# Deferred residual tails, joined super-tile halves and early loads in a two-layer encoder kernel on eight cores

## The chip, the cores and the metric

One Trainium2 chip, all eight cores, two sequences of the batch on each. A time is the device time of the slowest core, in microseconds (us). The kernels here have a second, slower state in some of their executions: the cores of one die or of both show a lower granted clock, and the time grows by some per cent. The granted clock is what the profile gives under that name, as a share of TensorE's full clock in a stretch. It is not low wherever PE is busy: from 1010 to 1200 us, in a dense FFN stretch of a fast run of the kernel before, it was 1.00 on each of the eight cores, with 217 ns a matmul (190.00 us for 874, core 5). An interval in brackets is a 95% interval. In profiles PE is TensorE, which does the matmuls, PEld its weight loads, DVE VectorE, ACT ScalarE, POOL GpSimd and SP the engine that issues the loads and stores.

## The reference

Two layers over x of 16 x 2048 x 1024. Layer 0 mixes tokens by windowed attention with rotary positions, layer 1 by a short gated convolution. Each is followed by a gated MLP ("FFN" below) whose gate goes through a width-3 convolution over positions. Every sub-layer has an RMSNorm before it and one after it, ahead of the residual add.

```python
def _dwconv3(x, w):                       # neighbours on both sides
    xp = jnp.pad(x, ((0, 0), (1, 1), (0, 0)))
    return xp[:, :-2] * w[0] + xp[:, 1:-1] * w[1] + xp[:, 2:] * w[2]

def _short_conv_mixer(h, w_in, conv_w, w_out):
    b_gate, c_gate, xv = jnp.split(h @ w_in, 3, axis=-1)
    return (b_gate * _dwconv3(c_gate * xv, conv_w)) @ w_out

def _conv_glu_ffn(h, w_gate_up, conv_w, w_down):
    g, u = jnp.split(h @ w_gate_up, 2, axis=-1)
    return (jax.nn.silu(_dwconv3(g, conv_w)) * u) @ w_down

def reference(x, positions, ...):
    ...
    for i in range(2):
        hn = _rmsnorm(h, g_pre_mix)
        mix = attention or conv mixer of hn           # cut
        h = h + _rmsnorm(mix, g_post_mix)
        f = _conv_glu_ffn(_rmsnorm(h, g_pre_ffn), ...)
        h = h + _rmsnorm(f, g_post_ffn)
    return h
```

## The kernel before

`h` of one sequence stays on chip as 8 channel tiles of 128 x 2048, float32. Work after attention goes in two halves ("super-tiles") of 1024 positions. A small scheduler records every instruction with the buffers it reads and writes, in program order, and turns that into semaphore waits; each engine gets its own instructions in that order. In the traces it also runs them so: in the kernel before the 32 VectorE instructions of a residual tail, from 944.85 to 967.33 us, alternate multiply and add as the program does. Weights stream through a ring of six slots, loaded by POOL. PSUM, the memory that matmuls write, is used as eight banks (`banks` in the kernel): six rotate (`poolA`) for products, banks 6 and 7 (`poolB`) serve norm sums. A super-tile begins with a barrier of all engines and queues, POOL's weight loads included:

```python
def barrier():
    toks = [...]                        # last instruction of PE, ACT, DVE; every DMA
    for e_ in ENGS:                     # all five, POOL too
        e_._waits(toks)

def proj_postnorm(units_fn, nk, mov, movB, xbuf, l, gj, st):
    ...
    for m in range(NCH):                # output blocks: matmuls, squares, copies
        ...
    for sub in range(2):                # the residual tail
        ...                             # rs = exp(-0.5 ln(mean square + eps))
        for m in range(NCH):
            hv = h[:, m, s0 + sub * 512: s0 + sub * 512 + 512]
            op(DVE, f_tt(xv[m][sub], xv[m][sub], rs.ap[:, :], ALU.mult), ...)
            op(DVE, f_tt(hv, hv, xv[m][sub], ALU.add), ...)
```

The width-3 convolution needs one position beyond the half, the "halo". The first half computes it as a one-column matmul beside each pair of 512-column ones. All eight halo slots are columns of bank 6 and share one buffer, so that a write waits for the last read of any of them:

```python
halo_slots = [Item(banks[6].ap[:, i:i + 1]) for i in range(8)]
for hs in halo_slots:
    hs.buf = banks[6].buf

def proj_halo(slot, hn, hnB, hc, with_halo=True):
    b0, b1 = poolA.next(), poolA.next()
    ...
    for k in range(NCH):
        w = slot.ap[:, k * 128:(k + 1) * 128]
        op(PE, f_mm(b0.ap[:, :], w, hn[k][:, 1:513], ...), ...)
        op(PE, f_mm(b1.ap[:, :], w, hn[k][:, 513:1025], ...), ...)
        if with_halo:
            op(PE, f_mm(hi.ap, w, hn[k][:, hc:hc + 1], ...), ..., [hi.buf])
    return b0, b1, hi
```

The gated convolution and the FFN, cut to the order of their instructions:

```python
def conv_layer():
    for st in range(2):
        barrier()
        ...
        hc = norm_super(l, 0, st, hn, hnB)
        for m in range(8):
            sx, sc, sb = ring_load(...), ring_load(...), ring_load(...)
            x0, x1, xh = proj_halo(sx, hn, hnB, hc, with_halo=(st == 0))
            ...                                     # ACT copies x0, x1, xh into xs
            c0, c1, ch = proj_halo(sc, hn, hnB, hc, with_halo=(st == 0))
            cx = cx_pool.next()
            op(DVE, f_tt(cx.ap[:, 1:513], c0.ap[:, :], xs.ap[:, 1:513], ALU.mult), ...)
            op(DVE, f_tt(cx.ap[:, 513:1025], c1.ap[:, :], xs.ap[:, 513:1025], ALU.mult), ...)
            if st == 0:
                op(DVE, f_tt(cx.ap[:, hc:hc + 1], ch.ap, xs.ap[:, hc:hc + 1], ALU.mult), ...)
                ...
            y = y_pool.next()
            conv3(y.ap, cx.ap, ...)
            b0, b1, _ = proj_halo(sb, hn, hnB, hc, with_halo=False)
            op(DVE, f_tt(yb[m][:, 0:512], y.ap[:, 0:512], b0.ap[:, :], ALU.mult), ...)
            op(DVE, f_tt(yb[m][:, 512:1024], y.ap[:, 512:1024], b1.ap[:, :], ALU.mult), ...)
        proj_postnorm(..., st)

def ffn_phase(l):
    for st in range(2):
        barrier()
        ...
        hc = norm_super(l, 2, st, hn, hnB)
        for j in range(NFF):                        # 22 column blocks
            ...                                     # gate and up products, ACT copies, conv3
            op(ACT, f_act(sl.ap[:, :], gc.ap[:, :], AF.Silu), ...)
            op(DVE, f_tt(actv[j][:, 0:512], sl.ap[:, 0:512], u0.ap[:, :], ALU.mult), ...)
            op(DVE, f_tt(actv[j][:, 512:1024], sl.ap[:, 512:1024], u1.ap[:, :], ALU.mult), ...)
        proj_postnorm(units_fn, NFF, actv, actB, xbuf, l, 3, st)
```

The softmax here doesn't subtract the row's maximum and nothing guards it: scores larger than these inputs give would overflow.

Of the kernel before, what the change touches and what calls it, by code (L numbers as in the profile page):

```python
# [15 lines left out]
NCH = 8  # L16
DFF = 2816
NFF = 22
# [176 lines left out]
def build_program(n_seq=2, stop_after=None, dbg_cols=0):  # L195
# [23 lines left out]
    SCRB = 112640  # L219
    with contextlib.ExitStack() as es:  # L220
# [75 lines left out]
        def barrier():  # L296
            toks = []
            for e_ in ENGS[:3]:
                if e_.cnt > 0:
                    toks.append((e_.sem, e_.cnt))  # L300
            for d in all_dsems:
                if d.cnt > 0:
                    toks.append((d.sem, d.cnt))
            for e_ in ENGS:
                e_._waits(toks)
# [4 lines left out]
        def norm_cols(src, srcB, gl, gj, dst, dstB, n):  # L310
            ssb = poolB.next()
# [13 lines left out]
        def proj_postnorm(units_fn, nk, mov, movB, xbuf, l, gj, st):  # L325
            s0 = st * 1024
            xv = [[xbuf[:, (m * 1024 + sub * 512):(m * 1024 + sub * 512 + 512)] for sub in range(2)]
                  for m in range(NCH)]
            xB = [[Buf() for _ in range(2)] for _ in range(NCH)]
            ssb = [banks[6], banks[7]]  # L330
# [8 lines left out]
            for m in range(NCH):  # L339
                slots = units_fn(m)  # L340
# [19 lines left out]
            while pend:  # L360
                flush(pend.pop(0))
            for sub in range(2):
                rs = rs_pool.next()
                op(ACT, f_act(rs.ap[:, :], ssb[sub].ap[:, :], AF.Ln, scale=1.0 / D, bias=epst[:, 0:1]),
                   [ssb[sub].buf, constB], [rs.buf])
                op(ACT, f_act(rs.ap[:, :], rs.ap[:, :], AF.Exp, scale=-0.5), [rs.buf], [rs.buf])
                tt = 2 * st + sub
                for m in range(NCH):
                    hv = h[:, m, s0 + sub * 512: s0 + sub * 512 + 512]
                    op(DVE, f_tt(xv[m][sub], xv[m][sub], rs.ap[:, :], ALU.mult), [xB[m][sub], rs.buf], [xB[m][sub]])  # L370
                    op(DVE, f_tt(hv, hv, xv[m][sub], ALU.add), [xB[m][sub], hB[m][tt]], [hB[m][tt]])

        def norm_super(l, gj, st, hn, hnB):
            s0 = st * 1024
            for sub in range(2):
                tt = 2 * st + sub
                src = [h[:, c, s0 + sub * 512: s0 + sub * 512 + 512] for c in range(NCH)]
                dst = [hn[c][:, 1 + sub * 512: 1 + sub * 512 + 512] for c in range(NCH)]
                norm_cols(src, [hB[c][tt] for c in range(NCH)], l, gj, dst, hnB, 512)
            if st == 0:  # L380
# [3 lines left out]
                norm_cols(src, [hB[c][tt] for c in range(NCH)], l, gj, dst, hnB, 1)  # L384
# [31 lines left out]
        def ffn_phase(l):  # L416
            for st in range(2):
                barrier()
                hn = [scr_bf(c * 2052, 1026) for c in range(NCH)]
                hnB = [Buf() for _ in range(NCH)]  # L420
                xbuf = scr_f32(0, 8192)
                A0 = 32832
                actv = [scr_bf(A0 + j * 2048, 1024) for j in range(NFF)]
                actB = [Buf() for _ in range(NFF)]
                G0 = A0 + NFF * 2048
                gs_pool = Pool_([Item(scr_f32(G0 + i * 4112, 1026)) for i in range(2)])
                G1 = G0 + 2 * 4112
                gc_pool = Pool_([Item(scr_f32(G1 + i * 4096, 1024)) for i in range(2)])
                G2 = G1 + 2 * 4096
                sl_pool = Pool_([Item(scr_bf(G2 + i * 2048, 1024)) for i in range(2)])  # L430
                hc = norm_super(l, 2, st, hn, hnB)
                zc = 1025 - hc
                for j in range(NFF):
# [19 lines left out]
                    op(DVE, f_tt(actv[j][:, 512:1024], sl.ap[:, 512:1024], u1.ap[:, :], ALU.mult), [sl.buf, u1.buf], [actB[j]])  # L453

                def units_fn(m):
                    r = []
                    for (k0, nkk) in ((0, 8), (8, 8), (16, 6)):
                        r.append((ring_load(wd[l, m, :, k0 * 128:(k0 + nkk) * 128], nkk * 128), nkk))
                    return r
                proj_postnorm(units_fn, NFF, actv, actB, xbuf, l, 3, st)  # L460

        def attn_layer(seq):
# [27 lines left out]
            qb_pool = Pool_([Item(scr_bf(U0 + i * 1024, 512)) for i in range(2)])  # L490
            t1_pool = Pool_([Item(scr_f32(U0 + 2048 + i * 2048, 512)) for i in range(2)])
            t2_pool = Pool_([Item(scr_f32(U0 + 6144 + i * 2048, 512)) for i in range(2)])
            tabB = Buf()
# [6 lines left out]
            for pc in range(4):  # L500
# [18 lines left out]
            barrier()  # L519
            if stop_after == 'rope':  # L520
                return dict(cos=cosT, sin=sinT)
            hnB = [Buf() for _ in range(8)]
            for tt in range(4):
                ts_ = slice(tt * 512, (tt + 1) * 512)
                src = [h[:, c, ts_] for c in range(8)]
                norm_cols(src, [hB[c][tt] for c in range(8)], 0, 0, hn_ap, hnB, 512)
                if stop_after == 'norm':
                    return dict(hn=hn_ap)
                for m in range(12):
                    slot = ring_load(wqk[m], 1024)  # L530
                    bk = poolA.next()
                    for k in range(8):
                        op(PE, f_mm(bk.ap[:, :], slot.ap[:, k * 128:(k + 1) * 128], hn_ap[k], k == 0, k == 7),
                           [slot.buf, hnB[k]], [bk.buf], inc=(k == 7))
                    qb = qb_pool.next()
                    op(ACT, f_act(qb.ap, bk.ap[:, :], AF.Copy), [bk.buf], [qb.buf])
                    t1 = t1_pool.next()
                    op(DVE, f_tt(t1.ap, bk.ap[:, :], cosT[:, ts_], ALU.mult), [bk.buf, tabB], [t1.buf])
# [8 lines left out]
                    op(DVE, f_tt(dst, t1.ap, t2.ap, ALU.add), [t1.buf, t2.buf], [dB])  # L547
                if stop_after == 'qk':
                    return dict(q0=[qrot[c][:, 0:512] for c in range(8)])
# [98 lines left out]
            xbuf = scr_f32(0, 8192)  # L648
            for st in range(2):
# [7 lines left out]
                proj_postnorm(lambda m: [(ring_load(wo[m], 1024), 8)], 8, mov, movB, xbuf, 0, 1, st)  # L657
                if st == 0:
                    barrier()
            return None  # L660

        def conv_layer():
            l = 1
            for st in range(2):
                barrier()
                hn = [scr_bf(c * 2052, 1026) for c in range(NCH)]
                hnB = [Buf() for _ in range(NCH)]
                A0 = 32832
                yb = [scr_bf(A0 + m * 2048, 1024) for m in range(8)]
                ybB = [Buf() for _ in range(8)]  # L670
                T0 = A0 + 16384
                xs_pool = Pool_([Item(scr_f32(T0 + i * 4112, 1026)) for i in range(2)])
                cx_pool = Pool_([Item(scr_f32(T0 + 8224 + i * 4112, 1026)) for i in range(2)])
                y_pool = Pool_([Item(scr_f32(T0 + 16448 + i * 4096, 1024)) for i in range(2)])
                hc = norm_super(l, 0, st, hn, hnB)
                zc = 1025 - hc
                for m in range(8):
                    sx = ring_load(win[16 + m], 1024)
                    sc = ring_load(win[8 + m], 1024)
                    sb = ring_load(win[m], 1024)  # L680
# [6 lines left out]
                    c0, c1, ch = proj_halo(sc, hn, hnB, hc, with_halo=(st == 0))  # L687
                    cx = cx_pool.next()
# [10 lines left out]
                    b0, b1, _ = proj_halo(sb, hn, hnB, hc, with_halo=False)  # L699
                    op(DVE, f_tt(yb[m][:, 0:512], y.ap[:, 0:512], b0.ap[:, :], ALU.mult), [y.buf, b0.buf], [ybB[m]])  # L700
                    op(DVE, f_tt(yb[m][:, 512:1024], y.ap[:, 512:1024], b1.ap[:, :], ALU.mult), [y.buf, b1.buf], [ybB[m]])
                xbuf = scr_f32(0, 8192)
                proj_postnorm(lambda m: [(ring_load(wout[m], 1024), 8)], 8, yb, ybB, xbuf, 1, 1, st)
# [12 lines left out]
        dump = None  # L716
        for seq in range(n_seq):
            for c in range(NCH):
                for hf in range(2):
                    dma(SP, f_dma(h[:, c, hf * 1024:(hf + 1) * 1024], xT[seq, c * 128:(c + 1) * 128, hf * 1024:(hf + 1) * 1024]),  # L720
                        [], [hB[c][2 * hf], hB[c][2 * hf + 1]], ld_sems[c][hf])
            dump = attn_layer(seq)
            if dump is not None:
# [3 lines left out]
            else:  # L727
                ffn_phase(0)
                if stop_after != "l0":
                    conv_layer()  # L730
                    if stop_after != "l1mix":
                        ffn_phase(1)
            for c in range(NCH):
                for hf in range(2):
                    dma(SP, f_dma(yT[seq, c * 128:(c + 1) * 128, hf * 1024:(hf + 1) * 1024], h[:, c, hf * 1024:(hf + 1) * 1024]),
                        [hB[c][2 * hf], hB[c][2 * hf + 1]], [], st_sems[c][hf])
# [16 lines left out]
        barrier()  # L753
# [104 lines left out]
```

## Time and profile before

| | before |
|---|---|
| time, median of 20 runs | 4318.04 us |
| PE busy, mean granted clock | 75%, 0.85 |
| one FFN half, PE without a gap | 235 to 240 us |
| one convolution layer, both halves | 290 us |
| gap between two halves of a stage | 32 to 42 us |
| gap between the sequences | 138 us |

In rows of instructions in order of time the columns are: start, length, engine and line, operation, tiles, shape, count, and in brackets the idle time before and what ended it.

### The profile page before, as it was taken

To read this page: it belongs to the slowest core of one execution; us is meant where nothing else is said; L and a number is where in the kernel's file an instruction comes from. 1 tells how busy PE (TensorE), PEld (TensorE's weight loads), DVE (VectorE), ACT (ScalarE), POOL (GpSimd) and SP (SyncE) were. 2 spreads that over 40 slices of the span, in tenths; PEclk is the share of its full clock that TensorE was granted. 3 is DMA by queue.
4 is the path that set the end of the run, shared out by engine and by line. 5 is a ranking of instruction groups with operands and counts; after the bars stand their busy time and mean duration, and the time that the engine had idled before them with its cause. 6 is when DMAs were issued, how large, how long until landed. Compare 5 with 4: busy or idle time off the path is not lost.

```text
span 4316.4 us, 50919 instructions; the slowest of 8 cores (4299.1 to 4316.4 us)
## 1 busy us (share of the span) xinstructions
PE 3251.2 (75%) x15616; PEld 1396.4 (32%) x15616; DVE 2060.6 (48%) x3177; ACT 1487.0 (34%) x2730; POOL 431.2 (10%) x820
## 2 busy tenths in 40 slices
PE   0666756979968769979506677669799688699795
PEld 0222222434423324424202222224344233244242
DVE  4554425626343646266145544266263446461651
ACT  1228833323222133233112288333232221332331
POOL 0110000111100101111001100011111001011110
PEclk9985577989979879989858855789899798899897
DMA  3430023535523425435434300235345234254354
GB/s 101 73 54 1 1 39 47 73 43 78 74 39 50 63 40 74 64 59 75 99 110 69 54 1 1 39 52 73 49 70 74 39 47 66 39 74 62 62 76 103
DMA packets 127418, 248.99 MB, mean 58 GB/s; under 512 B 14130, under 2 KB 22322, under 8 KB 126898
## 3 DMA queue, kind: packets, MB, share of 16 engines
q0 software_dynamic: 117504, 209.77, 33.1%
q1 hardware_dynamic: 9650, 35.97, 2.7%
q8 instruction: 134, 2.20, 0.2%
q14 instruction: 130, 1.06, 0.1%
HBM read 438.62 MB, written 16.78 MB: 106 GB/s over the span
## 4 chain that ended last, share of the span: by engine, by line
PE 70%; DVE 12%; ACT 9%; issue 5%; DMA 1%; SPq 1%; DVEq 0%; ACTq 0%; POOLq 0%
PE ps L157 70%; ACT scr L166 7%; DVE scr L170 5%; DVE h L170 4%; ACT rs L166 1%; DVE scr L180 1%; SPq L192 1%; DMA h<-xT 1%; DVE scr L175 1%; ACT sq L166 1%; DMA ring<-wo 0%; ACT L166 0%; DVEq L72 0%; ACTq L72 0%; DVE scr L184 0%
## 5 line engine op out<-in xcount | busy, mean ns | idle before, releaser
L157 PE MATMUL ps<-scr,ring 128*128 128x512 bf16 (+1 forms) x12736 | 2703.6, 370 | 167.2 <-DMA ring<-wo 74.8
L157 PEld LDWEIGHTS ps<-scr,ring 128*128 128x128 bf16 x12736 | 1186.3, 99 | 1631.4 <-issue 282.0
L166 ACT ACTIVATE scr<-ps 128x512 bf16<-128x512 f32 (+4 forms) x1256 | 650.2, 518 | 859.1 <-PE ps L157 778.5
L157 PE MATMUL ps<-sq,ones 128*128 128x512 bf16 (+1 forms) x560 | 209.8, 429 | 612.4 <-ACT sq L166 605.3
L170 DVE TENSOR_TENSOR scr<-scr,rs 128x512 f32<-128x512 f32 x256 | 175.8, 687 | 922.0 <-ACT rs L166 922.0
L180 DVE SCALAR_TENSOR_TENSOR scr<-scr,cst_sb 128x1024 f32<-128x1024 f32 x416 | 534.4, 1285 | 46.3 <-DVE scr L180 1.8
L166 ACT ACTIVATE scr<-scr 128x1024 bf16<-128x1024 f32 (+2 forms) x312 | 271.2, 869 | 720.1 <-DVE scr L180 657.3
L170 DVE TENSOR_TENSOR scr<-ps,scr 128x512 f32<-128x512 f32 (+1 forms) x528 | 281.9, 543 | 344.4 <-ACT scr L166 164.6
L170 DVE TENSOR_TENSOR scr<-scr,ps 128x512 bf16<-128x512 bf16 (+1 forms) x416 | 286.1, 688 | 271.6 <-PE ps L157 236.7
L166 ACT ACTIVATE sq<-ps 128x512 bf16<-128x512 f32 x256 | 153.0, 597 | 700.4 <-PE ps L157 668.0
L157 PE MATMUL ps<-scr 64*128 64x128 bf16 (+1 forms) x1840 | 275.2, 363 | 144.4 <-DVE scr L170 128.7
L192 POOL DMA_DIRECT2D ring<-wgu x352 | 185.9, 531 | 1433.0 <-PE ps L157 1047.2
L157 PEld LDWEIGHTS ps<-sq,ones 128*128 128x128 bf16 x560 | 55.9, 100 | 751.2 <-issue 723.2
L180 DVE SCALAR_TENSOR_TENSOR scr<-h,cst_sb,rs 128x512 bf16<-128x512 f32 (+1 forms) x304 | 178.8, 666 | 164.5 <-ACT rs L166 117.1
L166 ACT ACTIVATE sq<-h 128x512 bf16<-128x512 f32 (+1 forms) x304 | 142.9, 549 | 262.8 <-DVE h L170 261.2
L157 PEld LDWEIGHTS ps<-scr 64*128 64x128 bf16 (+1 forms) x1840 | 101.0, 128 | 308.1 <-issue 307.5
L170 DVE TENSOR_TENSOR h<-h,scr 128x512 f32<-128x512 f32 x256 | 177.3, 693 | 27.4 <-DVE scr L170 0.9
L166 ACT ACTIVATE scr<-ps,cst_sb 128x512 f32<-128x512 f32 x256 | 176.7, 690 | 0.1
L175 DVE TENSOR_SCALAR scr<-scr,cst_sb 128x1024 f32<-128x1024 f32 (+1 forms) x216 | 160.4, 743 | 24.2 <-DVE scr L188 1.6
L192 POOL DMA_DIRECT2D ring<-wd x192 | 101.3, 528 | 539.0 <-PE ps L157 538.9
L188 DVE MEMSET scr<- 128x1 f32 (+1 forms) x212 | 22.7, 107 | 216.7 <-ACT hsave L166 80.9
L170 DVE TENSOR_TENSOR scr<-scr,mlo 128x512 bf16<-128x512 bf16 x120 | 51.0, 425 | 150.8 <-ACT scr L166 150.8
(37 smaller groups left out, 709.4 us busy)
## 6 DMA issues: line engine op xcount, KB each, us to landing
ring<-wgu POOLq DMA_DIRECT2D x352, 256.0 KB, 3.8
ring<-wd POOLq DMA_DIRECT2D x128, 256.0 KB, 3.9
ring<-wqk POOLq DMA_DIRECT2D x96, 256.0 KB, 3.9
ring<-win POOLq DMA_DIRECT2D x96, 256.0 KB, 4.1
h<-xT SPq DMA_DIRECT2D x32, 512.0 KB, 19.2
yT<-h SPq DMA_DIRECT2D x32, 512.0 KB, 9.8
ring<-wd POOLq DMA_DIRECT2D x64, 192.0 KB, 3.6
ring<-wo POOLq DMA_DIRECT2D x32, 256.0 KB, 6.1
```

The lines of the kernel that those rows point to most:

```text
L157: return lambda e: e.matmul(out, lhsT=lhsT, rhs=rhs, start=start, stop=stop)
L166: return lambda e: e.activation(out=out, in_=in_, func=func, **kw)
L170: return lambda e: e.tensor_tensor(out=out, in0=in0, in1=in1, op=o)
L175: return lambda e: e.tensor_scalar(out=out, in0=in0, scalar1=s1, scalar2=None, op0=o0)
L180: return lambda e: e.scalar_tensor_tensor(out=out, in0=in0, scalar=scalar, in1=in1, op0=o0, op1=o1)
L188: return lambda e: e.memset(ap, v)
L192: return lambda e: e.dma_start(out=out, in_=in_)
```

## The change

It is meant to fill PE's gaps between halves. Residual tails become a list of closures that are emitted later, a few after each block of the next loop (`defer`, `drain`); the norm of the second half goes into the middle of the first half's last projection (`mid_hook`); the barrier between halves goes, and POOL no longer takes part in barriers; rotary tables are made piece by piece between tiles; the rotation matmul and the `b` product of the convolution lag by one block; the first half of the output is stored, and of the next sequence loaded, before the last down projection. Memory for `hn` moves so that it doesn't lie under the buffer of the deferred tail.

```diff
+        deferred = []
+        def drain(n=None):
+            k = len(deferred) if n is None else min(n, len(deferred))
+            for _ in range(k):
+                deferred.pop(0)()
+
+        def barrier(final=False):
+            drain()
 ...
             for e_ in ENGS:
+                if e_ is POOL and not final:
+                    continue
                 e_._waits(toks)
 ...                                                  # proj_postnorm
             for m in range(NCH):
+                if m == 4 and mid_hook is not None:
+                    while pend:
+                        flush(pend.pop(0))
+                    mid_hook()
 ...
+            def tail_pair(m, sub, rs):
+                def go():
+                    ...                               # the multiply and the add
+                return go
 ...
                 for m in range(NCH):
-                    op(DVE, ... ALU.mult)
-                    op(DVE, ... ALU.add)
+                    deferred.append(tail_pair(m, sub, rs))
+            if not defer:
+                drain()
 ...                                                  # FFN, end of each column block
                     op(DVE, f_tt(actv[j][:, 512:1024], sl.ap[:, 512:1024], u1.ap[:, :], ALU.mult), ...)
+                    drain(4)
 ...
+            hc = norm_super(l, 2, 0, hn, hnB)
+            gu_loop(0, hc)
+            hc1 = [0]
+            proj_postnorm(units_fn, NFF, actv, actB, xvb, l, 3, 0,
+                          mid_hook=lambda: hc1.__setitem__(0, norm_super(l, 2, 1, hn, hnB, ssp=poolA)), defer=True)
+            gu_loop(1, hc1[0])
+            if after_gu1 is not None:                 # store half 0, load half 0 of the next
+                drain()
+                after_gu1()
+            proj_postnorm(units_fn, NFF, actv, actB, xvb, l, 3, 1)
 ...                                                  # attention
+            rope_piece(0)
             for tt in range(4):
 ...
+                if tt < 3:
+                    rope_piece(tt + 1)
 ...
                 for m in range(12):
 ...                                                  # eight matmuls
+                    if lagq:
+                        rope_finish(lagq.pop(0))
 ...                                                  # ACT copy, DVE product with cos
+                    lagq.append((m, qb, t1))
 ...                                                  # convolution, both halves
+                def finish(item):
+                    m, y, sb = item
+                    b0, b1, _ = proj_halo(sb, hn, hnB, hc, with_halo=False)
+                    op(DVE, f_tt(yb[m][:, 0:512], y.ap[:, 0:512], b0.ap[:, :], ALU.mult), ...)
+                    op(DVE, f_tt(yb[m][:, 512:1024], y.ap[:, 512:1024], b1.ap[:, :], ALU.mult), ...)
 ...
                     c0, c1, ch = proj_halo(sc, hn, hnB, hc, with_halo=(st == 0))
+                    if lag:
+                        finish(lag.pop(0))
+                    sb = ring_load(win[m], 1024)
                     cx = cx_pool.next()
 ...                                                  # products of c and x, conv3
+                    lag.append((m, y, sb))
+                    drain(4)
```

The rest is memory offsets, plumbing and the halves' loads and stores.

## The prediction

What the terms called cold and table rest on: eight matmuls at 112.54 us took 3.62 us, at 140.99 us 1.89 us, so 1.73 more (the granted clock reads 1.00 in both stretches); the first eight after the gap at 940 us, from 981.50 to 984.70, took 3.19 us at a granted clock of 0.50 (cold and warm, here and in the expectations, name matmuls that are slow after a stop, as these, or not); an ACT_TABLE_LOAD took 1.28 us (20 loads), and at 942.04 us it was followed by Ln at 943.34.

> **What bounds the kernel now.** I read the page's head, the table by stage, the chain of waits around the gaps in that table, and the instructions in order of time inside one gap of each kind.
>
> ```profile
> span 4316.4 us, 50919 instructions; the slowest of 8 cores (4299.1 to 4316.4 us)
> ...
> PE 3251.2 (75%) x15616; PEld 1396.4 (32%) x15616; DVE 2060.6 (48%) x3177; ACT 1487.0 (34%) x2730; POOL 431.2 (10%) x820
> ```
>
> No engine is full over the whole span, so the stages decide. Columns of the table: stretch, its length, busy time of PE, PEld, DVE, ACT, POOL, granted clock, DMA share, GB/s.
>
> ```profile
> 98.00:320.00 222.00, 152.98 (x608) 60.66 (x608) 119.13 (x177) 57.36 (x104) 29.59 (x56) 0.92 0.45 67
> ...
> 591.00:623.00 32.00, 1.19 (x4) 0.38 (x5) 20.81 (x32) 3.93 (x7) 3.17 (x6) 0.58 0.11 15
> ...
> 700.00:940.30 240.30, 240.18 (x1246) 109.75 (x1246) 105.45 (x139) 72.09 (x141) 32.74 (x62) 0.99 0.47 66
> 940.30:981.50 41.20, 8.86 (x18) 1.88 (x19) 27.09 (x42) 16.59 (x29) 3.17 (x6) 0.59 0.22 39
> 981.50:1216.50 235.00, 234.99 (x1070) 104.96 (x1070) 109.02 (x139) 71.12 (x118) 32.72 (x62) 0.99 0.48 68
> ...
> 1395.20:1435.20 40.00, 9.22 (x20) 1.86 (x18) 27.06 (x42) 15.45 (x28) 3.17 (x6) 0.57 0.22 39
> ...
> 2114.20:2253.00 138.80, 0.76 (x3) 0.21 (x3) 66.33 (x117) 13.01 (x20) 0.25 (x1) 0.51 0.41 125
> ```
>
> The reader is to see two kinds of stretch. In a gated MLP (FFN) super-tile PE is full: 235.01/1070 = 220 ns per matmul, nothing to gain. Between super-tiles PE stands 32 to 46 us, and 139 us between the two sequences. The change aims at these. Inside the gap at 940 us:
>
> ```profile
> 941.59 0.38 PE L157 MATMUL ps<-sq,ones 128*128 128x512 bf16 x1 [0.69 <-ACT sq L166]
> ...
> 944.85 0.69 DVE L170 TENSOR_TENSOR scr<-scr,rs 128x512 f32<-128x512 f32 x1 [79.03 <-ACT rs L166]
> ...
> 967.75 4.27 ACT L166 ACTIVATE sq<-h 128x512 bf16<-128x512 f32 x8 [21.71 <-DVE h L170]
> ...
> 974.16 4.25 ACT L166 ACTIVATE sq<-h 128x512 bf16<-128x512 f32 x8
> ...
> 981.51 30.72 PE L157 MATMUL ps<-scr,ring 128*128 128x512 bf16 x132 [2.58 <-DVE scr L180]
> ```
>
> About 5 us of last squares, Ln and Exp; 22.4 us of residual tail (16 pairs of multiply and add, 1.40 us a pair); 14 us of next norm. Inside the FFN loop and in the query/key projection:
>
> ```profile
> 996.15 0.06 DVE L188 MEMSET scr<- 128x1 f32 x1
> ...
> 999.96 1.06 ACT L166 ACTIVATE scr<-scr 128x1024 bf16<-128x1024 f32 x1 [3.94 <-DVE scr L180]
> ...
> 1001.19 1.48 DVE L170 TENSOR_TENSOR scr<-scr,ps 128x512 bf16<-128x512 bf16 x2 [1.32 <-PE ps L157]
> ...
> 143.87 0.38 PE L157 MATMUL ps<-scr,pm 128*128 128x512 bf16 x1 [1.00 <-ACT scr L166]
> ```
>
> VectorE needs 996.15 to 1002.67, about 6.6 us per FFN column block, because it waits inside for the SiLU; PE needs 7.0. So VectorE has almost no room, although the table shows it 46% busy. In the projection PE waits 1.00 us per block for ScalarE's copy before the rotation matmul.
>
> [...]
>
> **The change part by part** (per sequence unless said).
>
> 1. *Rotary tables.* Before, all four pieces run ahead of the first norm: 39.3 to 97.3 us. After, one piece does (to about 55 us): -42.3. The other three do not vanish. Each sits in VectorE's queue between a tile's norm and its first rotation multiply; ScalarE's first copy waits behind the piece's Sin, so PE gets two blocks ahead and then stops. Each piece is about 14.9 us with a Sin table load.
> 2. *Lagged rotation matmul.* The period is 3.10 us per block; after it is the larger of PE 9 x 0.217 = 1.95 and VectorE three ops, about 2.05. For the last tile (no piece): from first square to the last value copy 7.9 (norm) + 6 (first block behind the norm) + 3.6 + 3.85 (two blocks cold) + 9 x 2.05 + 1.5 + 4.2 = 45.5, against 55.1: -9.6. A tile with a piece: 7.9 + 5.4 + 14.9 + (two cold blocks after the pause and eight warm ones, with the value projection: 29.2) + 0.5 = 58, against 55.1 (56.4 for the first, whose norm already loads a table): about +7 for three. The lag's gain is thus eaten by the pieces. Parts 1 and 2: -42.3 - 9.6 + 7 = about -45; I use -44.
> 3. *Output projection after attention.* POOL leaves the barriers, so weights are there at the start: -5 (553.23 to 558.32). Between its halves the barrier goes: 32 us, plus 2 us cold start, become the end of the squares (2) and one stall: the evacuation of block 0's second half into the shared buffer waits for tail pair 9, at 16 us, so PE stands about 5.5. 34 - 7.5: about -26.
> 4. *FFN, half 0 to half 1* (two per sequence). Before: 41.4 + 1.7 cold. After, the norm sits in the down projection, but PE still waits in order for its squares: 2.6 (block 3's evacuation) + 4.3 + 1.28 (table) + 1.4 + 4.3 + 0.5 = 14.4, + 1.7 cold. The tail goes to the gate/up loop, four pairs after each of the first four blocks: VectorE needs 6.6 + 5.6 = 12.2 us a block against PE's 7.0. The bank rotation lets PE start block j only when VectorE finished block j-2; its completions come at 13.4, 25.4, 37.4, 49.4, 61.6 us, so block 6 starts at 61.6 instead of 41.6: 20 us of stall, + 1.7 cold, + 2 at the end. Sum 39.8: only -3.3 each, -6.6.
> 5. *Gated convolution, half 0 to half 1.* Before 40.2 + 1.7. After: norm 13.1 (no table load) + 1.7 + end 1.7 + tail. PE takes 10.4 us a block here, VectorE 7.0 + 5.6 = 12.6: three stalls of 2 us. Sum 22.5: -19.4.
> 6. *Between the sequences*, once. Stores and loads took 2131.5 to 2188.9 us for 16.8 MB. Half of it moves under the last down projection; the other half needs some 28 us: -29. Against it: weights share the DMA engines with 8.4 MB. Their share there is 0.47 and the extra is about 29 us of full engines within 77 us, so it fits, but I charge +3.
> 7. *End*, once: eight stores after the tail, not sixteen: -13.
>
> Unchanged: attention (233 us), the FFN loops, and the three transitions per sequence (45 us each) that keep tail, barrier and norm.
>
> Sum: 2 x (44 + 5 + 26 + 6.6 + 19.4) = 202; 29 - 3 + 13 = 39; 241 in all. 4318 - 241 = 4077; I say 4075.
>
> **Rivals.** (a) *The deferred work is really hidden.* For it: VectorE is under 50% busy in the FFN stretches and the norm now lies amid matmuls. If so, FFN gives 25 more each (100 in all) and the tables 15 more a sequence: about 3950. Against it: 6.6 of 7.0 us[...]. (b) *New waits are worse.* Each drained block opens a 5 us gap on PE[...], and the early transfers delay weights. If PE falls cold throughout, FFN loses about 10 each and the projection 10 per sequence: about 4135. (c) *The projection becomes DMA-bound.* At 2.05 us per block, weights arrive at 256 KB/2.05 us = 125 GB/s, nearly twice 67 GB/s at share 0.45, so share about 0.84; for: little margin; against: six ring slots are refilled during the pieces. It would cost 5 to 10 a sequence: about 4090.
>
> **Range and chances.** Surest are the 42.3 us of part 1 and parts 3, 6 and 7: 2 x (42.3 + 31) + 39 = 186 together; the stalls in 2, 4 and 5, eight tile transitions or groups of them a sequence, may err by some 3 us each, about 50 either way in all. Range 4015 to 4125. Over 2% faster means below 4232, which needs two thirds of the sum to fail: 0.96 faster, 0.035 same, 0.005 slower.
>
> **What will show it.** Right: first matmul near 55 us, not 98; table loads 20 to 32; in the second FFN super-tile of each pair four PE gaps of about 5 us ending on VectorE after the multiplies, then none; 16 ones-matmuls in 14 us in mid down projection; no wait of PE for `wo`; first FFN super-tiles still 240 us; sequence gap 139 to about 66. Wrong: FFN halves joined without stalls (a), a second half over 265 us (b), or PE waiting for `wqk` (c). A lower granted clock in dense stretches on both dies would upset the sum altogether.

## More of the kernel before

Rows of the table by stage follow, for the convolution of the kernel before: the loop over the three products `x`, `c` and `b` of the first half, its output projection, and the loop of the second half. The columns are: stretch, length, busy time and number of instructions of PE, weight loads, DVE, ACT and POOL, granted clock, DMA share, GB/s.

```profile
1262.50:1367.60 105.10, 94.55 (x526) 42.33 (x526) 52.42 (x86) 10.94 (x24) 12.68 (x24) 0.97 0.41 61
1367.60:1395.20 27.60, 27.55 (x128) 12.42 (x128) 0.00 (x0) 15.93 (x29) 1.05 (x2) 1.00 0.14 20
1435.20:1525.20 90.00, 88.95 (x398) 39.14 (x399) 54.93 (x79) 9.58 (x16) 12.66 (x24) 0.98 0.49 71
```

The first half takes 15 us longer than the second, and its PE stands for 10 of its 105 us.

```profile
1282.81 11.09 PE L157 MATMUL ps<-scr,ring 128*128 128x1 bf16 x64 [1.11 <-ACT scr L166]
1286.18 1.75 DVE L170 TENSOR_TENSOR scr<-ps,scr 128x512 f32<-128x512 f32 x3 [4.70 <-PE ps L157]
1292.19 1.48 DVE L170 TENSOR_TENSOR scr<-scr,ps 128x512 bf16<-128x512 f32 x2 [0.17 <-PE ps L157]
```

A row gathers neighbouring instructions of one engine and names the shape of the first, so the 64 matmuls here are a whole block's: 24 for `x`, 24 for `c` and 16 for `b`, of them 16 for halo columns. PE stops once a block, for 1.11 us: the halo column of `c` goes to bank 6, and ScalarE must first have read that of `x` there. VectorE reads the second halo column of the block at 1286 to 1288 us, while PE is busy with the matmuls of `b`. Other than that, the shared bank stops PE nowhere in this block.

## The result, and the profile after

The changed kernel takes 4127.59 us (median of 10 runs, 4124.10 to 4131.87 but for one slow run of 4270.02) against 4318.04. The ratio is 0.9556 [0.9547, 0.9566]: 4.4% faster. A ratio here is the mean time of one kernel's fast runs over the mean of the other's fast runs of the same rounds, so it isn't quite the ratio of the medians. The gain is 190 us where 243 were predicted, and the time lies 2.6 us above the range. The head of the page of the kernel after:

```profile
span 4122.5 us, 50571 instructions; the slowest of 8 cores (4115.6 to 4122.6 us)
...
PE 3282.3 (80%) x15616; PEld 1403.9 (34%) x15616; DVE 2044.8 (50%) x3177; ACT 1498.3 (36%) x2742; POOL 432.8 (10%) x820
```

PE is 80% busy instead of 75%. The table by stage of the kernel after, with the columns as above: the query/key/value projection of the first sequence, one FFN's norm in the middle of the down projection and its second half, the three parts of the convolution, and the gap between the sequences:

```profile
68.50:279.00 210.50, 144.07 (x592) 60.83 (x592) 145.34 (x239) 68.78 (x117) 28.66 (x54) 0.81 0.46 68
...
830.50:845.00 14.50, 9.11 (x22) 2.07 (x21) 4.45 (x7) 13.14 (x23) 0.53 (x1) 0.76 0.19 30
...
886.00:1138.90 252.90, 239.04 (x1070) 105.24 (x1070) 125.03 (x164) 73.05 (x122) 35.82 (x67) 0.97 0.49 68
1185.90:1317.60 131.70, 102.26 (x526) 43.45 (x526) 51.79 (x87) 10.96 (x24) 12.74 (x24) 0.92 0.30 48
1317.60:1361.80 44.20, 38.83 (x146) 14.80 (x146) 10.79 (x16) 28.45 (x52) 4.22 (x8) 0.85 0.29 42
1362.00:1457.50 95.50, 88.23 (x399) 38.49 (x398) 70.05 (x104) 12.23 (x21) 12.72 (x24) 1.00 0.42 69
2041.10:2111.40 70.30, 0.75 (x2) 0.16 (x2) 34.66 (x54) 7.84 (x11) 0.46 (x1) 0.53 0.50 139
```

With the stages of both kernels laid side by side, each measured between landmarks such as the first square of a norm, the changes are these. The last column is (measured less predicted) times how often the stage occurs.

| stage (times it occurs) | before | after | change | predicted | miss in all |
|---|---|---|---|---|---|
| start to first norm square (1) | 97.3 | 68.5 | -28.8 | -42.3 | +13.5 |
| query/key/value projection (2) | 221.6 | 210.5 | -11.1 | -1.7 | -19 |
| start of the output projection (2) | | | -4.5 | -5 | +1 |
| its two halves (2) | 97 | 72 | -25 | -26 | +2 |
| FFN (4) | 516.4 | 508.9 | -7.5 | -3.3 | -17 |
| gated convolution (2) | 290.5 | 301.0 | +10.6 | -19.4 | +60 |
| between the sequences (1) | 137.7 | 70.3 | -67.4 | -68.3 | +1 |
| last matmul to the end (1) | 49.3 | 37.1 | -12 | -13 | +1 |

The misses sum to some 43 us, and the spans of the two traces differ by 47 us less than predicted (193.9 against 241), so the table holds nearly all of it. The convolution alone is +60. It got slower where the prediction had counted no change: the loop of its first half took 105.1 before and takes 131.7 after. (Its projection took 27.6 and takes 44.2 with the norm inside, and the loop of its second half 90.0 and 95.5, both as predicted.) The instructions of the first loop in order of time in the kernel after, somewhat more than a block:

```profile
1213.14 5.35 PE L157 MATMUL ps<-scr,ring 128*128 128x1 bf16 x24 [2.74 <-DVE scr L170]
1217.96 1.55 ACT L166 ACTIVATE scr<-ps 128x512 f32<-128x512 f32 x3 [15.06 <-PE ps L157]
1219.65 7.36 PE L157 MATMUL ps<-scr,ring 128*128 128x1 bf16 x40 [1.17 <-ACT scr L166]
1226.47 1.48 DVE L170 TENSOR_TENSOR scr<-scr,ps 128x512 bf16<-128x512 f32 x2 [9.39 <-PE ps L157]
1227.87 1.75 DVE L170 TENSOR_TENSOR scr<-ps,scr 128x512 f32<-128x512 f32 x3
...
1229.76 5.48 PE L157 MATMUL ps<-scr,ring 128*128 128x1 bf16 x24 [2.74 <-DVE scr L170]
```

One block now takes 16.62 us (1213.14 to 1229.76; 16.75 on average) instead of 12.25. A new wait of 2.74 us on VectorE has joined the old one of 1.17 on ScalarE, and the matmuls after it are slow: 24 in 5.35 us, where the same 24 of an earlier block, at 1198.06 us and after a stop of 1.39 us, took 3.87. The granted clock is 0.50 from 1213.0 to 1216.2 us, 1.00 from 1216.4 to 1229.9, and 0.50 again from 1230.1 to 1233.3. So a block pays twice for the new wait, 2.74 us for itself and some 1.5 us for slow matmuls.

The input of the first sequence also lands later. VectorE's first long fill, which waits at the opening barrier for it, starts at 35.28 us in the kernel before and 48.79 us in the kernel after:

```profile
35.28 3.47 DVE L188 MEMSET scr<- 128x4096 bf16 x1 [26.84 <-DMA h<-xT]
```

```profile
48.79 3.47 DVE L188 MEMSET scr<- 128x4096 bf16 x1 [40.29 <-DMA h<-xT]
```

On the eight cores the instant is 32.4 to 35.3 us before, and 42.5 to 48.8 after, 9 to 15 us later on each core and 12 on average. (Core 1, the slowest after, got it last.)

### The profile page after: what moved, and what is told of

Same layout as the page of the kernel before. It is cut to its first block, busy times and chain, and to the rows that moved or that the text cites. A ratio compares the mean times of both kernels' runs of the same rounds, so it can differ in the third digit from the quotient of the medians.

```text
span 4122.5 us, 50571 instructions; the slowest of 8 cores (4115.6 to 4122.6 us)
## 1 busy us (share of the span) xinstructions
PE 3282.3 (80%) x15616; PEld 1403.9 (34%) x15616; DVE 2044.8 (50%) x3177; ACT 1498.3 (36%) x2742; POOL 432.8 (10%) x820
## 3 DMA queue, kind: packets, MB, share of 16 engines
q0 software_dynamic: 117504, 209.77, 33.9%
## 4 chain that ended last, share of the span: by engine, by line
PE 66%; DVE 16%; ACT 9%; issue 6%; DMA 1%; SPq 1%; DVEq 0%; ACTq 0%; POOLq 0%
PE ps L157 66%; DVE scr L170 7%; ACT scr L166 6%; DVE scr L180 4%; DVE h L170 3%; DVE scr L175 1%; ACT sq L166 1%; ACT rs L166 1%; DMA h<-xT 1%; ACT L166 1%; SPq L192 1%; DVEq L72 0%; DVE scr L184 0%; DMA yT<-h 0%; ACTq L72 0%
## 5 line engine op out<-in xcount | busy, mean ns | idle before, releaser
L157 PE MATMUL ps<-scr,ring 128*128 128x512 bf16 (+1 forms) x12736 | 2743.0, 373 | 194.5 <-DVE scr L170 113.8
L157 PEld LDWEIGHTS ps<-sq,ones 128*128 128x128 bf16 x560 | 55.8, 100 | 527.8 <-issue 501.6
L166 ACT ACTIVATE sq<-h 128x512 bf16<-128x512 f32 (+1 forms) x304 | 143.0, 553 | 131.7 <-DVE h L170 130.4
```

What stands on the lines that cost most here:

```text
L157: return lambda e: e.matmul(out, lhsT=lhsT, rhs=rhs, start=start, stop=stop)
L166: return lambda e: e.activation(out=out, in_=in_, func=func, **kw)
```

## The experiments

All twelve kernels gave a correct result. "Before" times are of the same chip and rounds. Three groups of four ran on three chips. The kernel after was not run again with them; its 4127.6 us is set beside theirs, since the kernel before took 4315 to 4320 us in most fast runs of each group. Two of its runs count as fast though 1% above that: 4362.41 in the first group, which the mean of 4318 leaves out, and 4358.47 in the third, which the ratios there contain and which makes their intervals wide.

### The convolution

Theory H (halo): all halo columns share one bank and thus one buffer. The lag puts the two `b` products of the block before ahead of the `c` products in VectorE's queue, so bank 6 is read only after PE has finished the lagged matmuls, and PE's next halo column waits for that reading. Rival L: the lag itself costs it, by the later `b` matmuls and the ring slots they hold. Rival D: the deferred tails, the early barrier or the moved memory do it.

**e1: the kernel after, with no lag in the first half.**

```diff
                     lag.append((m, y, sb))
+                    if st == 0:
+                        finish(lag.pop(0))
                     drain(4)
```

> The lag of the third projection is undone in the first half of the gated convolution alone. Theory H (the lag puts the product that reads the halo's PSUM bank behind two multiplies that wait for PE, and PE's next halo matmul waits for that read): the block period there falls from 16.75 us to the 12.25 us of the kernel before, 26.5 us a sequence, so 4127 - 53 = 4074 us. Rival R (the half is slow because PE comes to it colder, or because weights are fetched across the barrier): no change, 4127 us.

Measured: 4068.9 us median of four, 4068.2 the mean of three fast runs against 4318, ratio 0.9423 [0.9404, 0.9441]. That is 59 us less than the kernel after, close to the expected 4074. A block takes 12.24 us again. From the first square of the convolution's norm to that of the next norm it takes 315.8 us, against 346.1 in the kernel after and 335.1 in the kernel before: 19.2 us less than before, where the prediction had 19.4. One row of its timeline, where the 2.74 us wait is gone and the old 1.17 is left:

```profile
1218.51 11.07 PE L157 MATMUL ps<-scr,ring 128*128 128x1 bf16 x64 [1.17 <-ACT scr L166]
```

So the loss against the prediction is the lag in the first half, all of it. Whether through the bank or by itself, e2 and e3 tell.

**e2: lag kept, halo columns of `c` in a bank of their own.** Bank 7 lies idle in this loop. Column `xh` stays in bank 6.

```diff
+        halo_slots7 = [Item(banks[7].ap[:, i:i + 1]) for i in range(8)]
+        for hs in halo_slots7:
+            hs.buf = banks[7].buf
...
-                    c0, c1, ch = proj_halo(sc, hn, hnB, hc, with_halo=(st == 0))
+                    c0, c1, ch = proj_halo(sc, hn, hnB, hc, with_halo=(st == 0), hslots=halo_slots7)
```

> The lag stays, but the halo column of the second projection goes to PSUM bank 7 instead of sharing bank 6 with the first one's. Theory H, shared bank: both waits on the bank go, that on VectorE (2.74 us) and that on ScalarE (1.17 us), and PE stays warm: the period falls to about 11 us, 8 x 5.7 us a sequence, so some 92 us in all: about 4036 us. Rival H2 (the lag itself starves PE of the six accumulation banks): period stays above 15 us, about 4120 us.

Measured: two fast runs, 4053.70 and 4054.46; the other two were slow, so there is no ratio. Against the fast runs of the kernel after that is about -74. The expected 4036 asked for 92, which was too much. The saving per block (16.75 less 10.92 is 5.83 us) would come to 93 only if all eight blocks of both sequences had it; the 37.4 us measured a sequence are 6.4 blocks' worth. The first block has no lagged product ahead of it; by the readings of the halo column, the first and the last of seven intervals fell by 2.8 and 4.2 us only. PE runs 217 matmuls, over three blocks' worth, without a stop, in the stretch where it stopped twice a block, and VectorE's `c` products, as late as ever, hold nobody up (timeline of e2):

```profile
1194.77 37.52 PE L157 MATMUL ps<-scr,ring 128*128 128x512 bf16 x217
...
1210.38 1.75 DVE L170 TENSOR_TENSOR scr<-ps,scr 128x512 f32<-128x512 f32 x3
```

A block takes 10.92 us. Here the lag is kept and the loss is gone, and with it the older wait on ScalarE. Rival L falls: in the loop of the first half the lag costs only through the shared bank. The kernel guards the halo columns by bank, with one buffer for all that lie there. No run here tries what happens without that guard; the runs show what it costs when two halo columns with different readers share a bank: waits of 2.74 and 1.17 us, and 16.75 us a block instead of 10.92.

**e3: lag kept, bank kept, only VectorE's order changed.** The lagged product goes behind the `c` products. PE's order stays.

```diff
                     c0, c1, ch = proj_halo(sc, hn, hnB, hc, with_halo=(st == 0))
-                    if lag:
-                        finish(lag.pop(0))
-                    sb = ring_load(win[m], 1024)
                     cx = cx_pool.next()
 ...                                                  # products of c and x
+                    if lag:
+                        finish(lag.pop(0))
+                    sb = ring_load(win[m], 1024)
                     y = y_pool.next()
```

> PE's order and the lag stay; VectorE's product with the halo is put ahead of the lagged multiplies in its queue. Theory H says the queue order is what makes PE wait: period back to 12.25 us or a little below, 4070 to 4080 us. If only the order of PE's matmuls mattered, no change: 4127 us.

Measured: fast runs 4054.74 to 4062.35, mean 4058.5, ratio 0.9400 [0.9384, 0.9416]. The block takes 12.24 us as in e1, with the same lag on PE as in the kernel after. So it is the place in VectorE's queue that makes the new wait. It beats the expected 4070 to 4080, since the second half gained as well, from 142.0 to 136.0 us (its loop and projection): PE waits for VectorE there in two blocks instead of three, and no longer at the start of the projection, where it had waited 2.14 us for the last lagged product.

**e4: the kernel before with nothing but the lag.** The convolution of the kernel before, barrier, memory and tails untouched, with `finish` and `lag` as in the diff.

```diff
+                def finish(item):
+                    m, y, sb = item
+                    b0, b1, _ = proj_halo(sb, hn, hnB, hc, with_halo=False)
+                    ...
                     c0, c1, ch = proj_halo(sc, hn, hnB, hc, with_halo=(st == 0))
+                    if lag:
+                        finish(lag.pop(0))
```

> The kernel before with nothing but the lag of the third projection. Theory H: first half of the convolution 26.5 us longer a sequence, second half (no halo) unchanged: 4318 + 53 = 4371 us. Rival R (it takes the rest of the change to make the half slow): 4318 us.

Measured: fast runs 4379.58 and 4377.32 against a mean of 4318, ratio 1.0141 [1.0117, 1.0166]; three other runs were slow. So +60 us, where +53 was expected. From norm to norm the first half grew by 27.9 us. The second, expected unchanged, grew by about 3: at the start of its projection PE waits 2.13 us instead of 1.00, for the last lagged product, and the 17 matmuls after that took 5.52 us, where 18 had taken 4.05. The wait in the first loop is there to the hundredth:

```profile
1306.60 5.49 PE L157 MATMUL ps<-scr,ring 128*128 128x1 bf16 x24 [2.74 <-DVE scr L170]
```

Rival D falls: the loss comes with the lag alone, without deferred tails, earlier weights or moved memory.

### The late input

Theory W: weights of the first projection, which POOL now loads without the opening barrier, share the DMA engines with the input and delay it. Theory O: the order of the input's loads (all of half 0, then all of half 1, instead of alternating) does it.

**e5: POOL takes part in the first barrier again.**

```diff
-            barrier()
+            barrier(final=(seq == 0))
```

> In the first sequence POOL waits at the opening barrier again, so no weights are fetched while the input is loaded. The input landed at 33 us before and at 42 to 48 us after. Theory W (the first six weight loads, fetched early, compete with the input): it lands at 33 us again, the kernel gains about 12 us: 4115 us. Rival O (the order by halves is slower): no change, 4127 us.

**e6: the old order of the input's loads.**

```diff
-                load_half(seq, 0)
-            load_half(seq, 1)
+                for c in range(NCH):
+                    for hf in range(2):
+                        dma(SP, ...)                  # as before
```

> The first input is loaded in the old order, both halves of a channel block in turn; weights are fetched early as in the changed kernel. Theory O: input lands at 33 us, 4115 us. Theory W: lands at 42 to 48 us still, 4127 us.

Measured: e5 4116.35 us median, all four runs fast, ratio 0.9533 [0.9516, 0.9549]; e6 two fast runs, 4128.26 and 4125.52, and three slow ones, ratio 0.9557 [0.9534, 0.9580], the same as the kernel after. The first rows of VectorE that wait for the input on core 0, of e5 and then of e6:

```profile
33.93 3.47 DVE L188 MEMSET scr<- 128x4096 bf16 x1 [26.08 <-DMA h<-xT]
```

```profile
45.52 3.47 DVE L188 MEMSET scr<- 128x4096 bf16 x1 [37.01 <-DMA h<-xT]
```

On all cores 33.9 to 36.4 us in e5, and 45.5 to 46.8 in e6. Theory W holds and O falls. From 10 to 32 us, while the input loads, the 16 DMA engines of a core are busy for 0.88 to 0.97 of the time in the kernel before, and for 0.99 or more on every core in the kernel after, where the weights are loaded beside it. For the six ring slots 6 x 128 x 1024 float32 are read, 3.1 MB, beside 8.4 MB of input: 37% more bytes for an input that lands a third later. For the first sequence the early weights buy nothing, since they aren't needed before the first norm is done.

### The deferred tail of the FFN

**e7: one pair per block, placed in VectorE's wait for SiLU.**

```diff
                     op(ACT, f_act(sl.ap[:, :], gc.ap[:, :], AF.Silu), [gc.buf], [sl.buf])
+                    drain(1)
                     op(DVE, f_tt(actv[j][:, 0:512], ...))
                     op(DVE, f_tt(actv[j][:, 512:1024], ...))
-                    drain(4)
```

> In the FFN loop one deferred pair per block is put between the convolution and the multiplies, where VectorE waits 1.32 us for the SiLU, instead of four pairs after each of the first four blocks. If the prediction's step on VectorE's queue is right, a pair of 1.40 us costs the queue about 0.1 us there, block time stays at PE's 7.0 us, the stalls of some 18 us vanish in each of four places: 4127 - 70 = 4057 us. Rival (the second half is slow for lack of VectorE time, whatever the place): 16 blocks at 8.0 us, about 4120 us.

**e8: one pair per block at the old place, the end of the block.**

```diff
-                    drain(4)
+                    drain(1)
```

> Control for the run above: one pair a block too, but after the multiplies as in the changed kernel. Queue theory: VectorE needs 6.6 + 1.4 = 8.0 us a block against PE's 7.0 for 16 blocks, 16 us of stall instead of 18: about 4120 us. If spreading alone were enough: about 4057 us as well.

First the kernel after, its second FFN half in order of time, with four pairs at the end of a block:

```profile
910.38 0.59 PE L157 MATMUL ps<-scr,ring 128*128 128x512 bf16 x1 [3.29 <-DVE scr L170]
...
922.43 0.38 PE L157 MATMUL ps<-scr,ring 128*128 128x512 bf16 x1 [2.02 <-DVE scr L170]
...
934.48 0.38 PE L157 MATMUL ps<-scr,ring 128*128 128x512 bf16 x1 [2.89 <-DVE scr L170]
...
946.53 0.49 PE L157 MATMUL ps<-scr,ring 128*128 128x512 bf16 x1 [4.33 <-DVE scr L170]
```

Then e7:

```profile
899.76 25.51 PE L157 MATMUL ps<-scr,ring 128*128 128x512 bf16 x116
...
905.45 0.68 DVE L170 TENSOR_TENSOR scr<-scr,rs 128x512 f32<-128x512 f32 x1
905.62 1.06 ACT L166 ACTIVATE scr<-scr 128x1024 bf16<-128x1024 f32 x1 [3.93 <-DVE scr L180]
906.24 0.69 DVE L170 TENSOR_TENSOR h<-h,scr 128x512 f32<-128x512 f32 x1
...
906.85 1.48 DVE L170 TENSOR_TENSOR scr<-scr,ps 128x512 bf16<-128x512 bf16 x2
```

While ScalarE computes SiLU from 905.62 to 906.68, VectorE does a multiply and an add of the tail, and its products begin at 906.85, as the add ends and 0.17 us after SiLU does; PE runs 116 matmuls without a stop. Measured: e7 two fast runs, 4046.62 and 4045.00, with two slow ones and no ratio; 82 us under the kernel after, better than the expected 4057. The stretch from the end of the mid norm to the end of the FFN fell from 293.9 to 273.4 us. e8: 4095.18, 4099.87 and 4102.50, ratio 0.9493 [0.9474, 0.9511]; that is -28 us, and the expected 4120 was missed. A block took 7.86 us there and not 8.0, and PE ran 129 matmuls, four blocks' worth, before it first waited:

```profile
917.97 7.45 PE L157 MATMUL ps<-scr,ring 128*128 128x512 bf16 x32 [0.41 <-DVE scr L170]
```

Of the 20.5 us an FFN that e7 gives back, spreading alone gives 7, and the place in the queue 13.

### The rotation lag, the mid norm and the tables

**e9: no lag of the rotation matmul.**

```diff
-                    if lagq:
-                        rope_finish(lagq.pop(0))
...
-                    lagq.append((m, qb, t1))
+                    rope_finish((m, qb, t1))
```

> The lag of the rotation matmul in the query/key projection is undone, the rotary pieces stay where the change put them. If the lag is what pays here: block period back from 2.0 us to 3.1 us, 10 to 11 us a tile, eight tiles: 4127 + 80 = 4207 us. If VectorE's three operations or the pieces set the pace (rival): under 4140 us.

Measured: fast runs 4239.19, 4244.65 and 4246.39, ratio 0.9795 [0.9711, 0.9879], which against the kernel before is called "unclear"; against the kernel after the difference is clear. The profiled run was slow, so only its undisturbed die is read. The lag is worth 116 us, 58 a sequence, and not the 80 that were expected. Without it a tile with a table piece takes 69 to 72 us (56 to 57 with it). Why a tile loses some 14 us and not 10 to 11 was not followed.

**e10: the norm of the second FFN half spread over the gate/up loop of the first,** one square per block on ScalarE, one ones-matmul a block later into bank 7, the rest after the loop; no norm within the down projection.

```diff
+            def spread():
+                if held:
+                    ones_mm()                         # one matmul, for the square of the block before
+                if todo:
+                    sub, c = todo.pop(0)
+                    sq = sq_pool.next()
+                    op(ACT, f_act(sq.ap[:, :], hsl(sub, c), AF.Square), ...)
+                    held.append((sub, c, sq))
-            gu_loop(0, hc)
+            gu_loop(0, hc, spread)                    # spread() at the end of each block
+            ...                                       # Ln, Exp and the multiplies for both subs
```

> In both FFNs the squares and ones-matmuls of the next half's norm are spread over the blocks of the first gate/up loop, one each a block, the matmul one block behind its square, into bank 7. If the norm amid the down projection costs PE its 14.4 us only because PE waits in order for the squares, PE's stop there vanishes but for 16 matmuls of 0.22 us: 4 x 11 to 13 us, about 4078 us. Rival: ScalarE has no room in the gate/up loop (its squares delay the SiLU and VectorE), first half of the FFN grows by as much: 4127 us.

Measured: 4084.34, 4091.91 and 4089.46 as fast runs, ratio 0.9442 [0.9325, 0.9560]; -39 us, about 10 of the 14.5 an FFN (expected 4078, so some 12).

**e11: all four table pieces of the first sequence made while its input loads.** The positions get a semaphore of their own and go ahead of the input; the first barrier goes.

```diff
-            barrier()
+            if seq > 0:
+                barrier()
...
+            dma(SP, f_dma(posi, posd[:, :]), [], [posB], pos_sem)
+            if seq == 0:
+                load_half(0, 0)
+                load_half(0, 1)
...
-            rope_piece(0)
+            for pc in range(4 if seq == 0 else 1):
+                rope_piece(pc)
...
-                if tt < 3:
+                if tt < 3 and seq > 0:
```

> In the first sequence the positions are loaded ahead of the input and all four rotary pieces run while the input lands. A tile with a piece took 56 to 57 us in the changed kernel, the tile without 41: if the pieces in VectorE's queue are the reason, three tiles lose 16 us each and the first norm still starts near 69 us: 4127 - 48 = 4079 us. If the tiles are slow for another reason (cold PE, weights), 4120 us or more.

Measured: 4081.3 us median, four fast runs of four, ratio 0.9420 [0.9359, 0.9481], as expected (4079). The first norm starts at 69.9 to 70.4 us on all cores, 2 to 8 us later than in the kernel after (62.3 to 68.5), and the tiles of the first sequence take 42.1, 40.9 and 41.1 us instead of 56 to 57. So a table piece between tiles costs 15 us, and in the load time less: three of them moved the start by those 2 to 8 us, or by 12 to 17 against the 53.6 to 58.0 us at which it comes when the weights wait (e5).

**e12: e2, e3, e7, e10 and e11 together, and two pairs instead of four per block in the convolution.**

> All repairs together: halo in its own bank, product first, two pairs a block in the convolution, one pair a block in the SiLU wait of the FFN, norm spread, tables in the load. If they add up: 4127 - 87 (convolution) - 82 (tail) - 50 (norm) - 48 (tables) = 3860 us. If spread norm and tail compete for the same waits of ScalarE and VectorE: some 20 us more.

Measured: five fast runs, 3863.65 to 3869.22, mean 3865.8, ratio 0.8923 [0.8875, 0.8972] (wide, because few runs of the kernel before were fast on that chip and one of these was 4358.47). That beats both kernels: 262 us under the kernel after, 452 under the kernel before. The convolution takes about 255 us and the FFN 478, where its matmuls alone take 475 (240.2 + 235.0 in the kernel before). The sum of the gains held to 6 us (3860 expected), though the convolution's share of it was an estimate: its three edits did not run together alone, nor did the two pairs a block. The page of e12:

```profile
span 3864.0 us, 50626 instructions; the slowest of 8 cores (3857.4 to 3864.0 us)
...
PE 3200.4 (83%) x15616; PEld 1395.2 (36%) x15616; DVE 2039.6 (53%) x3177; ACT 1494.4 (39%) x2740; POOL 444.7 (12%) x820
```

PE is busy for 82 us less than in the kernel after, with the same 15616 matmuls, which fits fewer of them running slowly after a stop; no run tests that alone.

## Why the prediction was right and where it was wrong

The direction was right, and the new waits of the FFN and the two projections were named ahead of the run; that of the convolution was not. The time missed the range, and by one step in the main.

1. *Rotary tables.* The step that failed in part: "one piece does (to about 55 us): -42.3". The first norm starts at 68.5. The table work was sized right (from the landing to the first norm 62.0 us before, 19.7 after, so -42.3), but part 1 took the landing as unchanged, and the early weights moved it by some 12 us (e5, e6). With the weights held back (e5) the first norm starts at 53.6 to 58.0 us, near the 55 of the prediction. Part 6 charged early loads 3 us between the sequences and nothing at the start. At the boundary itself -67.4 came of -68.3.
2. *Rotation lag.* The mechanism held: PE gets two blocks ahead of the table piece and stops (in the kernel after 16 matmuls from 134.15 us, then a stop of 12.91 us until ScalarE's copy, which follows the piece's second Sin at 153.68). The sizes were 58 us for a tile with a piece (measured 55.8 to 57.0) and 45.5 for the one without (41), so the projection came out 9 us a sequence better. "The lag's gain is thus eaten by the pieces" holds for the most part: three pieces cost 15 us each (e11), and the lag gains 58 a sequence (e9).
3. *Output projection.* -4.5 of -5 and -25 of -26; the stall was 5.11 us where 5.5 was predicted.
4. *FFN.* The mid norm takes 14.5 us (14.4 predicted). The tail made the second loop 18 us longer where 20 + 1.7 stood: a block with four pairs took 12.05 us and not 12.2, and PE's four gaps were 2.0 to 4.3 us and not about 5. The two microseconds charged to the end were 0.3. So an FFN gained 7.5 and not 3.3. e7 against e8 shows that the place in VectorE's order is why: with the same single pairs in the wait for SiLU, PE ran the 116 matmuls shown of e7 without a stop (25.51 us), and in e8 it waited for VectorE (0.41 us at 917.97).
5. *Gated convolution: this step failed.* The prediction put -19.4 and counted only the transition from half 0 to half 1. It did not follow the lag into the loop of the first half, which it left out as if unchanged. The terms that it had were right: the projection with the norm inside grew by 16.6 (13.1 + 1.7 + 1.7 predicted), the loop with the tail by 5.5 (6, and in three stalls as predicted), and the gap of 40 us went. But the first-half loop grew by 26.6 us, and this is 53 of the 60 us that the convolution missed by. The cause is shown from three sides: without the lag it goes (e1), with the lag alone it comes (e4), and with the lag kept it goes by another bank (e2) or another order on VectorE (e3). The rest of the 60 is the first half's lag too, since without it (e1) the convolution takes what the prediction said: PE waits 2.40 us for the last lagged product before the projection, instead of 1.40, and runs slowly after it, 18 matmuls in 5.73 us instead of 4.04.
6. *Between the sequences and the end.* -67.4 and -12, against -68.3 and -13.

Of the rivals, (a), that deferred work is hidden, is wrong for the kernel after, and e7, e10 and e11 show that it was a matter of place. (b), new waits with a cold PE, gave 4135 and lies nearest to the time, but for a reason it did not name: neither the FFN nor the projection lost, and the convolution did. It reckoned with slow matmuls after stops of 5 us. In the trace of the kernel after, whose matmul ends are modelled, the length of a stop alone does not tell whether they come: after stops of 2.74 us (convolution, 1213.14) and 2.02 us (FFN, 922.43) the granted clock was 0.50 (1213.0 to 1216.2 us, 922.8 to 925.4 us), and after one of 2.89 us (934.48) it stayed at 1.00 (934.4 to 937.6 us). (c), a projection bound by DMA, did not happen: blocks take about 2.0 us (1.94 in the last tile of the kernel after, 254.56 to 273.99 us). The chance of being 2% faster, 0.96, was well placed; the range was too narrow at its upper end, since it allowed some 3 us for each stall it had counted and nothing for a loop it hadn't looked at. That the total missed by only 53 us is in part luck: the convolution's +60 and the start's +13.5 met -36 from the projection and the FFN.

## What to carry to other kernels

When a change reorders a loop, list for every buffer which read frees it and what stands ahead of that read in its engine's queue, also for small things such as a one-column halo: the loop in which "nothing was removed" can pay for all that was gained elsewhere (here such a read, late in VectorE's queue, held PE for 2.74 us a block, and the loop grew by 26.6 us). Deferred work belongs in an engine's existing waits (behind the issue of another engine's long instruction), one piece at a time; put at a block's end it displaces the instructions that free the next engine's buffers (e7 took 82 us off the kernel after; e8, with the same pairs at the block's end, 28). Before loading early, ask what is needed sooner and shares the DMA engines: here the input, which landed some 12 us later (42.5 to 48.8 us, and 33.9 to 36.4 with the weights held back in e5).
